# Adding attention masks on VectorE in the pass that takes the row minimum, and giving the compressed keys a matmul in common with the local branch

## The chip, the cores and the metric

The kernel runs on one core of one Trainium2 chip. The metric is device time in microseconds (us) from launch to end of one execution; the median of several runs is compared. Engines are named as the profile names them: PE is TensorE (PEld its weight loads), DVE is VectorE, ACT is ScalarE, POOL is GpSimd and SP the engine that issues most transfers.

## What is computed

The program is a two-layer decoder trunk over 1024 tokens of width 1024. Layer 0 is a convolution path with memory attention, and an MLP. Layer 1 has three-branch sparse attention (NSA) with memory attention, and an MLP. The change lies in the three branches of layer 1. For a block c of 128 queries, t the query's position:

```python
s = einsum('bqghd,bngd->bqghn', qb, k_cmp) * scale             # compressed keys: 63, in 64 columns
p_cmp = masked_softmax(s, cmp_end[None, :] <= t[:, None])
...
smask = (top_val > -inf)[..., None] & (pos <= t[...])          # selected blocks
p = masked_softmax(s_selected, smask)
...
wmask = (kp <= t) & (kp > t - WIN) & (kp >= 0)                 # sliding window of 512
p = masked_softmax(s_window, wmask)
o = o_cmp * gate[0] + o_slc * gate[1] + o_win * gate[2]
```

With 16 blocks of 64 keys and 16 selected, the selected branch holds every key up to the query, so it is plain causal attention here.

## The kernel before

Tokens are worked on in two halves of 512 (`hf` 0 and 1). After layer 0 has been done for half 0, the program calls `attend(0)`, then the output projection and MLP of layer 0 for half 1, then `attend(1)`, and after it the output projection and MLP of layer 1 for both halves. Each `attend` ends in `nsa`, the stage that the change touches.

A scheduler lays out each engine's order when the program is built: it takes the steps in program order with estimated durations and lets independent ones pass. So the matmuls of an MLP (`mlp`: L441 to L443 into `ps_i`, L81 to L83 into `ps_mo`) stand between those of `nsa` on PE. Each engine then executes its row of instructions in that order.

`nsa` walks 8 memory-attention units and then 24 units per half: 2 key groups g, 4 query blocks c in descending order, 3 head pairs j. A unit has two heads i. `scores` computes one unit: for each head it multiplies the query by the keys. Every query is split into a high and a low part that fill the 128 rows, so each stretch of keys takes two matmuls (x is 0 or 1) into one bank of `ps_s` (three banks). The pieces of a unit are S (selected keys, at most 512 columns a piece: S0, S1), W (window keys: W0, W1) and C (64 compressed keys).

Masks are added on PE. `nsa_masks` builds `far` (128 columns, the window's far edge) and `dcm` (for each c 128 columns of diagonal mask, then 64 of compressed mask). A piece with a mask gets one more matmul into the same bank, with the identity `ident_r` as weights and the mask as the moving operand. In the pieces `dC` one mask matmul of 192 columns covers the window's diagonal and the compressed keys at once.

Then, for each piece, DVE takes the negated row maximum out of PSUM (L983), ACT does the exponential with it as bias, and sums the row (L987). After that DVE works out scale factors in the tile `small` (L990 to L1000) and POOL multiplies the probabilities by them (L1002, L1006). `values` then transposes the probabilities on PE (L1020), ACT and DVE split them into high and low parts (L1024, L1028), and PE multiplies them by V (L1036, L1039). The values of one unit follow the scores of the next.

The MLP's weights are prepared in slices of 128x512: a DMA brings a slice, ACT writes its high part (L109) and POOL its low part (L110).

Of the kernel before, what the change touches and what calls it, by code (L numbers as in the profile page):

```python
# [8 lines left out]
F32 = mybir.dt.float32  # L9
F32R = mybir.dt.float32r  # L10
# [853 lines left out]

def nsa_masks(k, far, dcm):

    nc = k.nc
    with k.tc.tile_pool(name="mb", bufs=1, side="right") as mp:  # L870
        z = mp.tile([P, P], F32, name="z")
        f = mp.tile([P, 2, P], F32, name="f")
        d = mp.tile([P, 8, 64], F32, name="d")
        nc.gpsimd.memset(z, 0.0)
        nc.gpsimd.affine_select(f[:, 0], z, [[1, P]], compare_op=ALU.is_ge, fill=NEG, base=-1, channel_multiplier=-1)
        nc.gpsimd.tensor_copy(far, f[:, 0])
        nc.gpsimd.affine_select(f[:, 1], z, [[-1, P]], compare_op=ALU.is_ge, fill=NEG, base=0, channel_multiplier=1)
        nc.gpsimd.tensor_copy(dcm[:, :, 0:P], f[:, 1:2].to_broadcast([P, 8, P]))
        nc.gpsimd.memset(d, NEG)
        for c in range(8):  # L880
            if c < 4:
                nc.gpsimd.affine_select(d[:, c, 0:31], z[:, :31], [[-16, 31]], compare_op=ALU.is_ge, fill=NEG,
                                        base=128 * c - 31, channel_multiplier=1)
            else:
                nc.gpsimd.memset(d[:, c, 0:31], 0.0)
                nc.gpsimd.affine_select(d[:, c, 32:64], z[:, :32], [[-16, 32]], compare_op=ALU.is_ge, fill=NEG,
                                        base=128 * c - 527, channel_multiplier=1)
        nc.gpsimd.tensor_copy(dcm[:, :, P:], d)


def nsa(k, pool, psum, hf, q, mq, gate, KcS, Vc, masks, Kd, Vd, kvd, pslot, mem_dst, out):


    nc = k.nc
    far, dcm = masks
    n = 4 * hf + 4
    outv = out.rearrange("(a p) k t -> p a k t", a=2)
    ring = [0]
# [38 lines left out]
    def scores(Q, c, g, j, KS, V):  # L937


        nb = min(c, 4) + 1  # L940
        Ws, Ww = (c + 1) * P, nb * P
        ko = (c + 1 - nb) * P
        h0 = 6 * g + 2 * j
        nm, ls, r, mn, f = small()
        sm = pool.tile([P, 2, 256], F32, tag="sm", name="sm", bufs=3)
        dia, cm = dcm[:, c, 0:P], dcm[:, c, P:]


        C = (KcS[:, g], sm[:, :, 128:192], [(0, cm)], 0)
        dC = (KcS[:, g], sm[:, :, 128:192], [(-P, dcm[:, c])], 0)  # L950
        if hf == 0:
            Sp, Wp = p4(), p4()
            S = (KS[:, 0, 0:Ws], Sp, [(Ws - P, dia)], 1)
            W = (KS[:, 1, 0:Ww], Wp, [(Ww - P, dia)] if c == 3 else [], 3)
            chunks = [[S, W, dC]] if c == 0 else [[S], [W, dC]] if c < 3 else [[S], [W], [C]]
            parts = [(Sp[:, :, :Ws], 0, 0), (Wp[:, :, :Ww], 1, 0)]
            sel = [Sp[:, :, b * P:(b + 1) * P] for b in range(c + 1)]
            win = [Wp[:, :, b * P:(b + 1) * P] for b in range(nb)]
        else:
            Sa, Wp, Sb = p4(), p4(), p4()  # L960
            S0 = (KS[:, 0, 0:HF], Sa, [], 1)
            S1 = (KS[:, 0, HF:Ws], Sb, [(Ws - HF - P, dia)], 2)
            W0 = (KS[:, 1, ko:ko + HF], Wp, [(0, far)], 3)
            W1 = (KS[:, 1, c * P:c * P + P], sm, [], 4)
            chunks = [[S0], [W0], [S1, W1, dC]] if c < 6 else [[S0], [S1], [W0], [W1, dC]]
            parts = [(Sa, 0, 0), (Sb[:, :, :Ws - HF], 0, 1), (Wp, 1, 0), (sm[:, :, 0:P], 1, 1)]
            sel = [(Sa if b < 4 else Sb)[:, :, b % 4 * P:b % 4 * P + P] for b in range(c + 1)]
            win = [Wp[:, :, b * P:(b + 1) * P] for b in range(4)] + [sm[:, :, 0:P]]
        for i in range(2):
            for chunk in chunks:  # L970
                ps = bank()
                mms, at, where = [], 0, []
                for keys, _, ms, _ in chunk:
                    w = keys.shape[-1]
                    mms += [(at, w, Q[:, x, i * P:(i + 1) * P], keys) for x in range(2)]
                    mms += [(at + a, m.shape[-1], k.ident_r, m) for a, m in ms]
                    where.append((at, at + w))
                    at += w
                for n_, (a, w, lhs, rhs) in enumerate(mms):
                    nc.tensor.matmul(ps[:, a:a + w], lhsT=lhs, rhs=rhs, start=(n_ == 0), stop=(n_ == len(mms) - 1))  # L980
                for (a, b), (_, dst, _, ix) in zip(where, chunk):
                    m = nm[:, ix, i:i + 1]
                    nc.vector.tensor_reduce(m, ps[:, a:b], axis=AX.X, op=ALU.max, negate=True)  # L983
                    if c == 0 and ix == 0:
                        nc.vector.tensor_scalar(m, m, 1e29, None, op0=ALU.min)
                    l = ls[:, ix, i:i + 1] if hf == 1 and ix else r[:, (ix + 1) // 2, i:i + 1]
                    nc.scalar.activation(dst[:, i, 0:b - a], ps[:, a:b], AF.Exp, bias=m, accum_out=l)  # L987
        if hf == 1:
            nv, lv = (t[:, 1:5].rearrange("p (b x) i -> p b x i", b=2) for t in (nm, ls))
            nc.vector.tensor_tensor(mn, nv[:, :, 0], nv[:, :, 1], op=ALU.min)  # L990
            nc.vector.tensor_sub(f, mn[:, :, None, :].to_broadcast([P, 2, 2, 2]), nv)
            nc.scalar.activation(f, f, AF.Exp)
            nc.vector.tensor_mul(lv, lv, f)
            nc.vector.tensor_add(r[:, 1:3], lv[:, :, 0], lv[:, :, 1])
# [50 lines left out]
    def units():  # L1045
        KS = pool.tile([P, 4, 256], F32R, tag="KS", name="KSm", bufs=1)
        V = pool.tile([P, 2, 4, P], F32R, tag="V", name="Vm", bufs=1)
        nc.sync.dma_start(KS.bitcast(F32), kvd[:, 0:1024].rearrange("p (h t) -> p h t", h=4))
        nc.sync.dma_start(V.bitcast(F32), kvd[:, 1024:2048].rearrange("p (t h d) -> p t h d", t=2, h=4))
        for cp in range(2):  # L1050
            for h in range(4):
                yield mem_query, mem_scores, (cp, h, KS, V)
        for g in range(2):
            KS = pool.tile([P, 2, 1024], F32R, tag="KS", name="KS", bufs=1)
            V = pool.tile([P, 2, 8, P], F32R, tag="V", name="V", bufs=1)
            nc.sync.dma_start(KS[:, :, :n * P].bitcast(F32), Kd[:, g, :, :n * P])
# [57 lines left out]
def build(tc, ins, out):  # L1114
# [11 lines left out]
    with ExitStack() as es:  # L1126
# [4 lines left out]
        nc.sync.dma_start(k.cols, ins["cols"])  # L1131
        k.ident = cp.tile([P, P], F32, name="ident")
        make_identity(nc, k.ident)
        k.ident_r = cp.tile([P, P], F32R, name="ident_r")
        nc.gpsimd.tensor_copy(k.ident_r, k.ident)
        k.ones = cp.tile([P, P], F32, name="ones")
        nc.gpsimd.memset(k.ones, 1.0)
        halves = cp.tile([P, 24], F32, name="halves")
# [91 lines left out]

        ka = K()
        ka.nc, ka.tc, ka.i = nc, tc, ins
        ka.cols, ka.rows, ka.ident, ka.ident_r, ka.ones = k.cols, k.rows, k.ident, k.ident_r, k.ones
        ka.mqg, ka.kng = k.mqg, k.kng
        ka.lo_eng = nc.vector
        ka.nraw, ka.nhl, ka.tag, ka.nps, ka.nc_, ka.nt_ = NRAWA, NHLA, "a", 4, 3, 2
# [122 lines left out]
```

## Time and profile before

| what | value |
|---|---|
| median of 3 runs | 2488.69 us (2487.76 to 2490.86) |
| the profiled execution | 2490.74 us |
| its span, first to last instruction | 2488.9 us |
| mean granted PE clock | 0.987 of full speed |
| PE busy | 2410.1 us, 97% of the span, 12566 matmuls |
| DVE busy | 1667.7 us, 67%, 3270 instructions |
| ACT busy | 1294.0 us, 52% |
| POOL busy | 1223.6 us, 49% |

The profile's busy time is the union of an engine's records. A matmul's record is longer than the time by which it delays the next one, since matmuls overlap; what one costs is read from the chain of waits, which lists how much each piece moves the end. Line numbers are those of the kernel before unless said otherwise.

### The profile page before, as it was taken

To read this page: it belongs to the slowest core of one execution; us is meant where nothing else is said; L and a number is where in the kernel's file an instruction comes from. 1 tells how busy PE (TensorE), PEld (TensorE's weight loads), DVE (VectorE), ACT (ScalarE), POOL (GpSimd) and SP (SyncE) were. 2 spreads that over 40 slices of the span, in tenths; PEclk is the share of its full clock that TensorE was granted. 3 is DMA by queue.
4 is the path that set the end of the run, shared out by engine and by line. 5 is a ranking of instruction groups with operands and counts; after the bars stand their busy time and mean duration, and the time that the engine had idled before them with its cause. 6 is when DMAs were issued, how large, how long until landed. Compare 5 with 4: busy or idle time off the path is not lost.

```text
span 2488.9 us, 37416 instructions
## 1 busy us (share of the span) xinstructions
PE 2410.1 (97%) x12566; PEld 2043.2 (82%) x12566; DVE 1667.7 (67%) x3270; ACT 1294.0 (52%) x2938; POOL 1223.6 (49%) x1044
## 2 busy tenths in 40 slices
PE   7997999999998999999999999999999999999999
PEld 5886788888787888888787898888888887888887
DVE  7898587987778666766436866777777655433333
ACT  5565555333545466665334545666666644333332
POOL 3675743556632356464445325555555542444443
PEclk9998999999999999999999999999999999999999
DMA  6311433232444242322335434212222124332323
GB/s 212 100 50 53 140 104 104 93 101 92 140 140 130 89 117 69 89 70 84 109 102 164 145 112 125 82 57 59 71 80 60 56 82 147 119 97 93 98 94 102
DMA packets 157791, 250.91 MB, mean 101 GB/s; under 512 B 17696, under 2 KB 49056, under 8 KB 157088
## 3 DMA queue, kind: packets, MB, share of 16 engines
q1 hardware_dynamic: 157600, 248.52, 32.2%
q8 instruction: 100, 1.64, 0.3%
q14 instruction: 91, 0.75, 0.1%
HBM read 217.52 MB, written 20.45 MB: 96 GB/s over the span
## 4 chain that ended last, share of the span: by engine, by line
PE 64%; DVE 4%; DMA 2%; issue 1%; ACT 1%; POOL 1%; SPq 0%; ACTq 0%; DVEq 0%; POOLq 0%
PE ps_mo L81 7%; PE ps_i L441 7%; PE ps_i L443 7%; PE ps_i L442 7%; PE ps_mo L83 7%; PE ps_mo L82 7%; PE ps_s L980 6%; PE ps_t L1020 4%; PE ps_o L1036 2%; PE ps_o L1039 2%; PE ps_tok L666 1%; PE ps_tok L668 1%; PE ps_tok L667 1%; PE ps_wo L400 1%; PE ps_wo L402 1%
## 5 line engine op out<-in xcount | busy, mean ns | idle before, releaser
L110 POOL TENSOR_TENSOR hl<-raw,hl 128x512 fp32r<-128x512 f32 x592 | 771.4, 1313 | 938.3 <-ACT hl L109 901.5
L109 ACT ACTIVATE hl<-raw 128x512 fp32r<-128x512 f32 x656 | 409.8, 630 | 647.5 <-PE ps_mo L83 248.3
L463 DVE TENSOR_TENSOR x<-x,ps_mo 128x512 f32<-128x512 f32 x512 | 348.5, 683 | 157.0 <-PE ps_mo L83 154.2
L81 PE MATMUL ps_mo<-hid,hl 128*128 128x512 f32 x1024 | 410.9, 402 | 9.2 <-DVE a L449 5.6
L441 PE MATMUL ps_i<-act,hl 128*128 128x512 f32 x1024 | 406.3, 397 | 8.5 <-DVE x L404 6.9
L442 PE MATMUL ps_i<-act,hl 128*128 128x512 f32 x1024 | 404.5, 395 | 1.2 <-DVE act L410 1.2
L443 PE MATMUL ps_i<-act,hl 128*128 128x512 f32 x1024 | 404.8, 396 | 0.0
L83 PE MATMUL ps_mo<-hid,hl 128*128 128x512 f32 x1024 | 402.8, 393 | 0.0
L82 PE MATMUL ps_mo<-hid,hl 128*128 128x512 f32 x1024 | 402.2, 393 | 0.0
L81 PEld LDWEIGHTS ps_mo<-hid,hl 128*128 128x128 f32 x1024 | 193.0, 189 | 51.9 <-DVE x L463 7.8
L441 PEld LDWEIGHTS ps_i<-act,hl 128*128 128x128 f32 x1024 | 193.3, 189 | 48.4 <-DVE x L404 7.3
L442 PEld LDWEIGHTS ps_i<-act,hl 128*128 128x128 f32 x1024 | 193.1, 189 | 42.5 <-DVE act L410 2.2
L83 PEld LDWEIGHTS ps_mo<-hid,hl 128*128 128x128 f32 x1024 | 192.9, 188 | 41.0
L443 PEld LDWEIGHTS ps_i<-act,hl 128*128 128x128 f32 x1024 | 193.1, 189 | 40.6 <-issue 0.2
L82 PEld LDWEIGHTS ps_mo<-hid,hl 128*128 128x128 f32 x1024 | 193.2, 189 | 37.0 <-issue 0.7
L449 DVE SCALAR_TENSOR_TENSOR a<-ps_i,r 128x512 f32<-128x512 f32 x128 | 87.9, 688 | 196.4 <-PE ps_i L443 192.0
L983 DVE TENSOR_REDUCE small<-ps_s 128x1 f32<-128x512 f32 (+4 forms) x384 | 164.0, 442 | 51.8 <-PE ps_s L980 35.9
L987 ACT ACTIVATE prob<-ps_s,small 128x512 f32<-128x512 f32 (+3 forms) x240 | 141.1, 589 | 98.8 <-DVE small L983 96.6
L1028 DVE TENSOR_TENSOR PT<-ps_t,PT 128x512 fp32r<-128x512 f32 (+1 forms) x220 | 146.8, 671 | 65.9 <-ACT PT L1024 64.6
L1006 POOL TENSOR_TENSOR prob<-prob,small 128x1024 f32<-128x1024 f32 (+3 forms) x120 | 180.9, 1532 | 1.1 <-DVE small L1000 0.7
L1024 ACT ACTIVATE PT<-ps_t 128x512 fp32r<-128x512 f32 (+1 forms) x256 | 140.8, 566 | 69.9 <-PE ps_t L1020 65.7
L980 PE MATMUL ps_s<-KS,Q 128*128 128x512 f32 (+3 forms) x576 | 148.3, 349 | 0.0
(299 smaller groups left out, 4781.9 us busy)
## 6 DMA issues: line engine op xcount, KB each, us to landing
raw<-in_w_mlp_in_dram SPq DMA_DIRECT2D x256, 256.0 KB, 2.7
raw<-in_w_mlp_out_dram SPq DMA_DIRECT2D x256, 256.0 KB, 2.8
raw<-in_w_out_dram SPq DMA_DIRECT2D x64, 256.0 KB, 3.0
Q<-Q SPq DMA_DIRECT2D x160, 64.0 KB, 2.0
raw<-in_cmp_w_dram SPq DMA_DIRECT2D x32, 256.0 KB, 2.7
raw<-in_a_w_dram SPq DMA_DIRECT2D x24, 256.0 KB, 2.8
raw<-in_b_wq_dram SPq DMA_DIRECT2D x24, 256.0 KB, 2.7
mixd<-ev SPq DMA_DIRECT2D x80, 64.0 KB, 2.1
```

The lines of the kernel that those rows point to most:

```text
L81: nc.tensor.matmul(ps, lhsT=lh, rhs=rh, start=(i == 0), stop=False)
L82: nc.tensor.matmul(ps, lhsT=lh, rhs=rl, start=False, stop=False)
L83: nc.tensor.matmul(ps, lhsT=ll, rhs=rh, start=False, stop=(i == n - 1))
L109: nc.scalar.activation(hl[:, 0, :n], raw[:, :n], AF.Copy)
L110: k.last_lo = k.lo_eng.tensor_tensor(hl[:, 1, :n], raw[:, :n], hl[:, 0, :n].bitcast(F32), op=ALU.subtract)
L441: nc.tensor.matmul(p_, lhsT=wh, rhs=h[kt][:, 0], start=kt == 0, stop=False)
L442: nc.tensor.matmul(p_, lhsT=wh, rhs=h[kt][:, 1], start=False, stop=False)
L443: nc.tensor.matmul(p_, lhsT=wl, rhs=h[kt][:, 0], start=False, stop=kt == KT - 1)
L463: nc.vector.tensor_add(x[o], x[o], ps)
L980: nc.tensor.matmul(ps[:, a:a + w], lhsT=lhs, rhs=rhs, start=(n_ == 0), stop=(n_ == len(mms) - 1))
L983: nc.vector.tensor_reduce(m, ps[:, a:b], axis=AX.X, op=ALU.max, negate=True)
L1006: nc.gpsimd.tensor_tensor(t, t, sc[:, :, None].to_broadcast([P, 2, t.shape[-1]]), op=ALU.mult)
```

## The change

Masks go to DVE. A masked piece is now handled by one operation, `tensor_tensor_reduce`: it reads scores from PSUM and a mask from SBUF, writes minus their sum back to the same place of PSUM, and takes the minimum of the row (starting from 1e29) into `small`. The exponential then reads the negated scores with scale -1. In the instruction stream the operation is two instructions: the pass itself (`ISA ps_s,small<-ps_s,...`) and a second one that writes the row's result (`ISA small 128x1`). Pieces without a mask keep the plain reduction.

`edge` holds both 128-column masks in one f32 tile of 640 columns: far, then 384 columns of zeros, then the diagonal, so a slice of it gives a mask as wide as the piece. `cm` holds the compressed masks. `ident_r`, and the casts of masks for PE, are gone.

The window's keys in `KS` are followed by 64 compressed keys, which POOL copies there at the first head pair of each (g, c) (16 copies); c descends, so the block that they overwrite is no longer needed. W and C are then one moving operand. For c of 0 and 4 a strided operand also takes the diagonal block of the selected keys, with 64 columns between them that are computed and not read.

```diff
-        dia, cm = dcm[:, c, 0:P], dcm[:, c, P:]
-        C = (KcS[:, g], sm[:, :, 128:192], [(0, cm)], 0)
-        dC = (KcS[:, g], sm[:, :, 128:192], [(-P, dcm[:, c])], 0)
+        win0 = 1024
+        last = KS[:, win0 + c * P:win0 + c * P + P + 64]
+        if j == 0:
+            nc.gpsimd.tensor_copy(last[:, P:], KcS[:, g])
+        C = (64, sm[:, :, 128:192], cm[:, c], 0)
         if hf == 0:
...
-            chunks = [[S, W, dC]] if c == 0 else [[S], [W, dC]] if c < 3 else [[S], [W], [C]]
+            chunks = [[(KS[:, 0:Ws], [S])]]
+            chunks += [[(KS[:, win0:win0 + Ww + 64], [W, C])]] if c < 3 else [
+                [(KS[:, win0:win0 + Ww], [W])], [(last[:, P:], [C])]]
         else:
...
-            chunks = [[S0], [W0], [S1, W1, dC]] if c < 6 else [[S0], [S1], [W0], [W1, dC]]
+            chunks = [[(KS[:, 0:HF], [(HF, Sa, None, 1)])], [(KS[:, win0 + ko:win0 + ko + HF], [W0])]]
+            end = [(KS[:, HF:Ws], [S1]), (last, [W, C])]
+            chunks += [end] if c == 5 else [end[:1], end[1:]]
...
+        if c % 4 == 0:
+            both = KS[:, 0:2 * win0].rearrange("p (a t) -> p a t", a=2)[:, :, c * P:c * P + P + 64]
+            chunks[0 if hf == 0 else 2:] = [[(both, [tri, (64, None, None, None), W, C])]]
...
-                    mms += [(at + a, m.shape[-1], k.ident_r, m) for a, m in ms]
...
-                    nc.vector.tensor_reduce(m, ps[:, a:b], axis=AX.X, op=ALU.max, negate=True)
-                    if c == 0 and ix == 0:
-                        nc.vector.tensor_scalar(m, m, 1e29, None, op0=ALU.min)
+                    if mask is None:
+                        nc.vector.tensor_reduce(m, s, axis=AX.X, op=ALU.max, negate=True)
+                    else:
+                        nc.vector.tensor_tensor_reduce(s, s, mask, -1.0, 1e29, ALU.add, ALU.min, m)
                     l = ls[:, ix, i:i + 1] if hf == 1 and ix else r[:, (ix + 1) // 2, i:i + 1]
-                    nc.scalar.activation(dst[:, i, 0:b - a], ps[:, a:b], AF.Exp, bias=m, accum_out=l)
+                    nc.scalar.activation(dst[:, i, 0:w], s, AF.Exp, bias=m, scale=1.0 if mask is None else -1.0, accum_out=l)
```

Counted over the instruction streams, the score matmuls go from 1020 to 552. Of 576 on keys, 192 on compressed keys and 252 on masks there remain 264 of 512 columns (unchanged), 24 of 448, 96 of 384, 24 of 320, 48 of 256, 72 of 192 and 24 of 64. On DVE 336 of the 384 reductions become pairs (144 in half 0, 192 in half 1), and 12 small `tensor_scalar` go.

Three places show how the order moves. The first is PE in half 1, a unit of c = 6, one head: its S1 (384 columns), W0, W1 and C. Before:

```order
L980 MATMUL ps_s<-KS,Q 128x384 x2
L980 MATMUL ps_s<-dcm,ident_r 128x128
L980 MATMUL ps_s<-KS,Q 128x512 x2
L980 MATMUL ps_s<-far,ident_r 128x128
L980 MATMUL ps_s<-KS,Q 128x128 x2
L980 MATMUL ps_s<-KcS_2539,Q 128x64 x2
L980 MATMUL ps_s<-dcm,ident_r 128x192
```

The same pieces of such a unit after the change (`ps_o` and `ps_t` belong to the unit before it):

```order
L989 MATMUL ps_s<-KS,Q 128x512 x2
L1052 MATMUL ps_o<-PT,V 128x256
L1049 MATMUL ps_o<-PT,V 128x256
L1052 MATMUL ps_o<-PT,V 128x256
L1033 MATMUL ps_t<-ident,prob 128x128 x4
L989 MATMUL ps_s<-KS,Q 128x384 x2
L989 MATMUL ps_s<-KS,Q 128x192 x2
```

Eleven matmuls have become six. Between the first and the last score matmul of half 0 the order now has 615 MLP matmuls of 512 columns where it had 534, and in half 1 it has 1091 where it had 961; after the last one 2023 PE rows remain, before 2156.

The second place is DVE in half 1, at a unit of c = 4. Before, with the split of transposed probabilities (L1028) between the reductions:

```order
L1028 TENSOR_TENSOR PT<-ps_t,PT 128x512
L983 TENSOR_REDUCE small<-ps_s 128x1
L1028 TENSOR_TENSOR PT<-ps_t,PT 128x512
L983 TENSOR_REDUCE small<-ps_s 128x1 x2
L1028 TENSOR_TENSOR PT<-ps_t,PT 128x512
L983 TENSOR_REDUCE small<-ps_s 128x1
```

After (S0 has no mask, W0 has the far mask, S1 the diagonal):

```order
L1041 TENSOR_TENSOR PT<-ps_t,PT 128x512
L995 TENSOR_REDUCE small<-ps_s 128x1
L449 SCALAR_TENSOR_TENSOR a<-ps_i,r 128x512
L998 ISA ps_s,small<-ps_s,edge 128x512
L998 ISA small 128x1
L998 ISA ps_s,small<-ps_s,edge 128x128
L998 ISA small 128x1
```

Each masked piece takes two places in the queue where it took one.

The third place is POOL in half 1, where a new query block begins. Such a copy had no counterpart before:

```order
L1019 TENSOR_TENSOR prob<-prob,small 128x1024
L1019 TENSOR_TENSOR sm<-sm,small 128x2x128
L110 TENSOR_TENSOR hl<-raw,hl 128x512 x2
L945 COPY KS<-KcS_2537 128x64
L1015 TENSOR_TENSOR sm<-sm,small 128x2x64
```

The copy waits for PE (the last window matmul of the block before) and stands behind two preparations of weights; the first window matmul of the new block waits for it.

## Rows read from the trace of the kernel before

**Rows 1.** The page: busy us of the engines, and PE in 40 slices.

```profile
PE 2410.1 (97%) x12566; PEld 2043.2 (82%) x12566; DVE 1667.7 (67%) x3270; ACT 1294.0 (52%) x2938; POOL 1223.6 (49%) x1044
...
PE   7997999999998999999999999999999999999999
```

**Rows 2.** Windows, the two attention stages: us, then busy us of PE, PEld, DVE, ACT, POOL.

```profile
911.00:1136.00 225.00, 225.00 (x1383) 200.19 (x1382) 163.39 (x383) 155.99 (x456) 125.24 (x126) 1.00 0.27 77
1556.00:1998.00 442.00, 442.00 (x2669) 390.50 (x2667) 328.95 (x734) 293.17 (x818) 251.32 (x219) 1.00 0.22 66
```

**Rows 3.** Chain of waits: its shares by line, then pieces: start, us, what.

```profile
by line: PE ps_mo L81 6.8%; PE ps_i L441 6.7%; PE ps_i L443 6.7%; PE ps_i L442 6.6%; PE ps_mo L83 6.6%; PE ps_mo L82 6.6%; PE ps_s L980 5.7%; PE ps_t L1020 4.2%; PE ps_o L1036 2.3%; PE ps_o L1039 2.1%; PE ps_tok L666 1.4%; PE ps_tok L668 1.
...
1133.04 1.54 PE ps_s L980 x14
...
1566.68 1.10 PE ps_s L980 x8
...
1699.52 0.46 PE ps_s L980 x2
1699.98 0.23 PE ps_mo L81
1700.21 0.53 PE ps_s L980 x3
1700.74 0.28 PE ps_mo L82
...
1701.48 0.88 PE ps_s L980 x8
```

**Rows 4.** Groups by form, DVE from 1560 to 2000 us: count, busy us, mean ns.

```profile
L1028 DVE TENSOR_TENSOR PT<-ps_t,PT 128x512 fp32r<-128x512 f32 x119 | 81.3, 685 | 38.1 <-ACT PT L1024 37.3
L983 DVE TENSOR_REDUCE small<-ps_s 128x1 f32<-128x512 f32 x105 | 71.6, 683 | 17.9 <-PE ps_s L980 17.3
L463 DVE TENSOR_TENSOR x<-x,ps_mo 128x512 f32<-128x512 f32 x80 | 54.3, 680 | 8.4 <-PE ps_mo L83 7.5
L89 DVE TENSOR_TENSOR hid<-a,hid 128x512 fp32r<-128x512 f32 x20 | 17.4, 872 | 9.2 <-ACT hid L88 8.8
L983 DVE TENSOR_REDUCE small<-ps_s 128x1 f32<-128x128 f32 x59 | 16.4, 283 | 8.1 <-PE ps_s L980 6.5 <-ACT prob L987 1.4
L449 DVE SCALAR_TENSOR_TENSOR a<-ps_i,r 128x512 f32<-128x512 f32 x20 | 13.7, 683 | 3.8 <-PE ps_i L443 3.7
...
L983 DVE TENSOR_REDUCE small<-ps_s 128x1 f32<-128x64 f32 x46 | 9.9, 216 | 4.4 <-ACT sm L987 4.2
```

**Rows 5.** Timeline of DVE, then of ACT, from 1700 us: start, us, engine, line.

```profile
1700.94 0.69 DVE L1028 TENSOR_TENSOR PT<-ps_t,PT 128x512 fp32r<-128x512 f32 x1
1701.54 0.68 DVE L983 TENSOR_REDUCE small<-ps_s 128x1 f32<-128x512 f32 x1
1702.14 0.68 DVE L1028 TENSOR_TENSOR PT<-ps_t,PT 128x512 fp32r<-128x512 f32 x1
...
1703.45 0.69 ACT L987 ACTIVATE prob<-ps_s,small 128x512 f32<-128x512 f32 x1 [3.20 <-DVE small L983]
1704.04 0.19 ACT L987 ACTIVATION_READ_ACCUMULATOR prob<-ps_s,small 128x1 f32 x1
1704.16 0.69 ACT L987 ACTIVATE prob<-ps_s,small 128x512 f32<-128x512 f32 x1
```

**Rows 6.** Waits from 1560 to 2000 us: total us, times, longest us.

```profile
POOL hl L110 <- ACT hl L109: 144.0, 37, 8.9
ACT prob L987 <- DVE small L983: 65.7, 56, 4.3
```

**Rows 7.** Groups by form: preparation of a weight slice, and a small POOL pass.

```profile
L110 POOL TENSOR_TENSOR hl<-raw,hl 128x512 fp32r<-128x512 f32 x592 | 771.4, 1313 | 938.3 <-ACT hl L109 901.5 <-issue 33.0 <-DVE nt L97 1.8
...
L109 ACT ACTIVATE hl<-raw 128x512 fp32r<-128x512 f32 x656 | 409.8, 630 | 647.5 <-PE ps_mo L83 248.3 <-PE ps_i L443 244.3 <-PE ps_wo L402 26.9
...
L1002 POOL TENSOR_TENSOR sm<-sm,small 128x128 f32<-128x128 f32 x96 | 41.0, 428 | 93.2 <-DVE small L998 73.8 <-PE ps_s L226 5.7 <-ACT PT L1024 5.3
```

More of the change, by code (lines that the diff above doesn't have):

```diff
@@ L862, in kv_tok, with nsa_masks @@
     k.pe(850)
-def nsa_masks(k, far, dcm):
+def nsa_masks(k, edge, cm):
     nc = k.nc
[L870 to L888, printed above, removed]
+    z = edge[:, P:2 * P]
+    nc.gpsimd.memset(edge[:, P:4 * P], 0.0)
+    nc.gpsimd.affine_select(edge[:, 0:P], z, [[1, P]], compare_op=ALU.is_ge, fill=NEG, base=-1, channel_multiplier=-1)
+    nc.gpsimd.affine_select(edge[:, 4 * P:], z, [[-1, P]], compare_op=ALU.is_ge, fill=NEG, base=0, channel_multiplier=1)
+    nc.gpsimd.memset(cm, NEG)
+    for c in range(8):
+        if c < 4:
+            nc.gpsimd.affine_select(cm[:, c, 0:31], z[:, :31], [[-16, 31]], compare_op=ALU.is_ge, fill=NEG,
+                                    base=128 * c - 31, channel_multiplier=1)
+        else:
+            nc.gpsimd.memset(cm[:, c, 0:31], 0.0)
+            nc.gpsimd.affine_select(cm[:, c, 32:64], z[:, :32], [[-16, 32]], compare_op=ALU.is_ge, fill=NEG,
+                                    base=128 * c - 527, channel_multiplier=1)
 def nsa(k, pool, psum, hf, q, mq, gate, KcS, Vc, masks, Kd, Vd, kvd, pslot, mem_dst, out):
     nc = k.nc
-    far, dcm = masks
+    edge, cm = masks
     n = 4 * hf + 4
@@ L945, in scores @@
         sm = pool.tile([P, 2, 256], F32, tag="sm", name="sm", bufs=3)
-        dia, cm = dcm[:, c, 0:P], dcm[:, c, P:]
-        C = (KcS[:, g], sm[:, :, 128:192], [(0, cm)], 0)
-        dC = (KcS[:, g], sm[:, :, 128:192], [(-P, dcm[:, c])], 0)
+        win0 = 1024
[3 more added lines that the diff above has]
+        C = (64, sm[:, :, 128:192], cm[:, c], 0)
         if hf == 0:
             Sp, Wp = p4(), p4()
-            S = (KS[:, 0, 0:Ws], Sp, [(Ws - P, dia)], 1)
-            W = (KS[:, 1, 0:Ww], Wp, [(Ww - P, dia)] if c == 3 else [], 3)
-            chunks = [[S, W, dC]] if c == 0 else [[S], [W, dC]] if c < 3 else [[S], [W], [C]]
+            S = (Ws, Sp, edge[:, 5 * P - Ws:], 1)
+            W = (Ww, Wp, edge[:, 5 * P - Ww:], 3)
             parts = [(Sp[:, :, :Ws], 0, 0), (Wp[:, :, :Ww], 1, 0)]
@@ L958, in scores @@
             win = [Wp[:, :, b * P:(b + 1) * P] for b in range(nb)]
+            chunks = [[(KS[:, 0:Ws], [S])]]
+            chunks += [[(KS[:, win0:win0 + Ww + 64], [W, C])]] if c < 3 else [
+                [(KS[:, win0:win0 + Ww], [W])], [(last[:, P:], [C])]]
+            tri = S
         else:
             Sa, Wp, Sb = p4(), p4(), p4()
[L961 to L964, printed above, removed]
-            chunks = [[S0], [W0], [S1, W1, dC]] if c < 6 else [[S0], [S1], [W0], [W1, dC]]
+            S1 = (Ws - HF, Sb, edge[:, 5 * P - Ws + HF:], 2)
+            W0 = (HF, Wp, edge[:, 0:HF], 3)
+            W = (P, sm, edge[:, 4 * P:], 4)
+            chunks = [[(KS[:, 0:HF], [(HF, Sa, None, 1)])], [(KS[:, win0 + ko:win0 + ko + HF], [W0])]]
+            end = [(KS[:, HF:Ws], [S1]), (last, [W, C])]
+            chunks += [end] if c == 5 else [end[:1], end[1:]]
             parts = [(Sa, 0, 0), (Sb[:, :, :Ws - HF], 0, 1), (Wp, 1, 0), (sm[:, :, 0:P], 1, 1)]
@@ L968, in scores @@
             win = [Wp[:, :, b * P:(b + 1) * P] for b in range(4)] + [sm[:, :, 0:P]]
+            tri = S1
+        if c % 4 == 0:
+            both = KS[:, 0:2 * win0].rearrange("p (a t) -> p a t", a=2)[:, :, c * P:c * P + P + 64]
+            chunks[0 if hf == 0 else 2:] = [[(both, [tri, (64, None, None, None), W, C])]]
         for i in range(2):
@@ L971, in scores @@
                 ps = bank()
[L972 to L975, printed above, removed]
-                    mms += [(at + a, m.shape[-1], k.ident_r, m) for a, m in ms]
[L977 to L982, printed above, removed]
-                    nc.vector.tensor_reduce(m, ps[:, a:b], axis=AX.X, op=ALU.max, negate=True)
-                    if c == 0 and ix == 0:
-                        nc.vector.tensor_scalar(m, m, 1e29, None, op0=ALU.min)
+                at, mms, where = 0, [], []
+                for keys, pieces in chunk:
+                    b = at
+                    for piece in pieces:
+                        where.append((b, piece))
+                        b += piece[0]
+                    out_ = ps[:, at:b]
+                    if len(keys.shape) == 3:
+                        out_ = out_.rearrange("p (a t) -> p a t", a=2)
+                    mms += [(out_, Q[:, x, i * P:(i + 1) * P], keys) for x in range(2)]
+                    at = b
+                for n_, (o_, lhs, rhs) in enumerate(mms):
+                    nc.tensor.matmul(o_, lhsT=lhs, rhs=rhs, start=(n_ == 0), stop=(n_ == len(mms) - 1))
+                for a, (w, dst, mask, ix) in where:
+                    if dst is None:
+                        continue
+                    m, s = nm[:, ix, i:i + 1], ps[:, a:a + w]
+                    if mask is None:
+                        nc.vector.tensor_reduce(m, s, axis=AX.X, op=ALU.max, negate=True)
+                    else:
+                        nc.vector.tensor_tensor_reduce(s, s, mask, -1.0, 1e29, ALU.add, ALU.min, m)
                     l = ls[:, ix, i:i + 1] if hf == 1 and ix else r[:, (ix + 1) // 2, i:i + 1]
-                    nc.scalar.activation(dst[:, i, 0:b - a], ps[:, a:b], AF.Exp, bias=m, accum_out=l)
+                    nc.scalar.activation(dst[:, i, 0:w], s, AF.Exp, bias=m, scale=1.0 if mask is None else -1.0, accum_out=l)
         if hf == 1:
@@ L1053, in units @@
         for g in range(2):
-            KS = pool.tile([P, 2, 1024], F32R, tag="KS", name="KS", bufs=1)
+            KS = pool.tile([P, 2 * 1024 + 64], F32R, tag="KS", name="KS", bufs=1)
+            kv2 = KS[:, 0:2048].rearrange("p (b t) -> p b t", b=2)
             V = pool.tile([P, 2, 8, P], F32R, tag="V", name="V", bufs=1)
-            nc.sync.dma_start(KS[:, :, :n * P].bitcast(F32), Kd[:, g, :, :n * P])
+            nc.sync.dma_start(kv2[:, :, :n * P].bitcast(F32), Kd[:, g, :, :n * P])
             nc.sync.dma_start(V[:, :, :n].bitcast(F32), Vd[:, g, :, :n])
@@ L1133, in build @@
         make_identity(nc, k.ident)
-        k.ident_r = cp.tile([P, P], F32R, name="ident_r")
-        nc.gpsimd.tensor_copy(k.ident_r, k.ident)
         k.ones = cp.tile([P, P], F32, name="ones")
@@ L1199, in build @@
         tail = late.tile([P, 4, 8], F32, name="tail")
-        masks = (late.tile([P, P], F32R, name="far"), late.tile([P, 8, 192], F32R, name="dcm"))
+        masks = (late.tile([P, 5 * P], F32, name="edge"), late.tile([P, 8, 64], F32, name="cm"))
         xp = pool(es, "x")
@@ L1232, in build @@
         ka.nc, ka.tc, ka.i = nc, tc, ins
-        ka.cols, ka.rows, ka.ident, ka.ident_r, ka.ones = k.cols, k.rows, k.ident, k.ident_r, k.ones
+        ka.cols, ka.rows, ka.ident, ka.ones = k.cols, k.rows, k.ident, k.ones
         ka.mqg, ka.kng = k.mqg, k.kng
```

## The prediction

> **What bounds the kernel now.** I read the page first, then the windows of the two stages that the change touches, then the chain of waits there. The page shows PE busy for 97% of the span and in nearly every slice [rows 1]. The windows say more: from the first score matmul to the last, 225 us in half 0 and 442 us in half 1, PE has no idle time at all, while DVE is busy for 163.4 and 329.0 us of them [rows 2]. The reader is to see that what keeps PE occupied there is not only attention: the order puts MLP matmuls between the pieces, so PE always has something to do. The chain of waits runs along PE through both stages, and 5.7% of it, some 142 us, is the line of the score matmuls [rows 3]. So work taken off PE there comes off the end, as long as the other engines still feed it. That is the whole argument, and DVE is the engine to watch, since it gets the work.
>
> **What PE loses.** The chain gives the price of a matmul as the time by which it moves the next. A 512-column one costs 0.23 us, two 0.46 [rows 3], which is 0.45 ns per column. A narrow one costs far more than its columns: fourteen of 64 to 192 columns in a row take 1.54 us, 0.11 each; two of 512 and six narrow ones take 1.10, again 0.11 for a narrow one; two of 256 and six narrow ones take 0.88. A single mask matmul behind two wide ones shows as 0.07 (0.53 less 0.46), but the wide matmul behind it then costs 0.28, so 0.12 in all [rows 3]. I price all widths up to 192 at 0.11 and the others by columns: 0.115 for 256, 0.144 for 320, 0.173 for 384, 0.202 for 448.
>
> Before, besides the 264 of 512 columns that stay: 612 narrow ones, 67.3 us; 72 of 256, 8.3; 72 of 384, 12.4; together 88.0 us. After: 24 of 448, 4.8; 96 of 384, 16.6; 24 of 320, 3.5; 48 of 256, 5.5; 96 narrow, 10.6; together 41.0 us. PE loses 47 us, about 19 in half 0 and 28 in half 1. As a check, the prices give 264 x 0.23 + 88.0 = 149 us for the line before, where the chain has 142. If all the difference lies in the narrow ones they cost 0.10 and the gain is 41 us. I keep 47 and hold 41 as its near end. The order agrees with a full PE: the scheduler fills the freed room with 81 and 130 more MLP matmuls, and those are missing later. Some 300 MLP matmuls of half 0 are still left behind the last unit, so the stage that follows keeps its cover.
>
> [...] The rows have a narrow matmul at 0.11 us [rows 3]. [...]
>
> **What DVE gains.** 336 reductions become a pass with two inputs and a readout. The pass: for 512 columns the reduction takes 683 ns and the nearest operation with one input in PSUM and one in SBUF takes 685 [rows 4], and in the timeline both follow each other at 0.60 us [rows 5]. So I take the pass at the reduction's price. The readout has no row on DVE. On ACT the same thing, an accumulator read behind the exponential, is a record of 0.19 us that delays the next instruction by 0.12 [rows 5]. I call the extra price per masked piece d and take d = 0.12. Its low end is 0: both forms read the same columns, and nothing suggests that the new one could be cheaper. Its high end is a sum and a reduction done one after the other. A reduction delays the next by its record less 0.08 (0.60 of 0.683 [rows 4, 5]), so 0.60, 0.20 and 0.14 us for 512, 128 and 64 columns; over the mix of half 1 the second pass is 0.33 on average, and with 0.15 for a readout as an operation of its own d = 0.48.
>
> [...]
>
> Room on DVE: the MLP's own DVE work comes to 54.3 + 17.4 + 13.7 us [rows 4] for 961 matmuls, 0.089 each, so the extra MLP matmuls add 7.2 us in half 0 and 11.6 in half 1. Free are then 225 - 163.4 - 7.2 = 54 us for 144 pieces, d = 0.38, and 442 - 329.0 - 11.6 = 101 us for 192, d = 0.53 [rows 2]. At d = 0.12 DVE gets 17 and 23 us, and is 83% busy. So it is hidden behind PE. But PE takes its row in a fixed order: a late maximum delays the exponential, and ACT already waits for DVE there 56 times, 4.3 us at the longest [rows 6]. If a bank of scores or a transposed block is late, PE stands. I charge 4 us for such stands; nothing in the trace prices them, and PE has none now.
>
> **The other edits.** ACT's count is unchanged. Sixteen copies on POOL cost at most 0.43 us each by a pass twice as wide [rows 7], and POOL is idle for 100 us in half 0 and 191 in half 1 [rows 2]. The transfers are the same. The copy adds a wait: the first window matmul of a block waits for POOL, and the copy stands behind weight preparations, which themselves wait for ACT, 8.9 us at the longest [rows 6]. About fifty PE rows lie between the matmul that frees the columns and the one that needs them, 8 us or so at 0.16 us each (442 us for 2669 [rows 2]), so I take it as hidden.
>
> **The sum.** 2490.7 - 47 + 4 = 2448 us for the profiled execution. The median of the runs is 2 us below that execution, so **2446 us** is the forecast, 1.7% faster. Each rival below is on the median's scale too.
>
> **Rivals.**
> - **DVE fills up in half 0.** With d = 0.48 half 0 has 144 x 0.48 = 69 us to place in 54, so 15 us come back, and half 1 is nearly full, with some 2 us of stands more: about 2463. For: DVE is the busiest of the three feeding engines, and nothing bounds a pass that writes PSUM and reads it. Against: the two-input row costs what the reduction costs.
> - **DVE becomes the bound and it is slower.** Per 0.1 of d over both limits 33.6 us come back. The gain of 47 is gone at 336 d - 155 = 47, d = 0.60. At d = 0.75, which is the second pass, the readout and 0.27 us more per pair, 49 us are lost: about 2538. For: the instruction is of a kind that the trace does not have, and most masked pieces are small, so a fixed cost per instruction would weigh twice. Against: a reduction of 64 columns takes 0.216 us in all [rows 4], so the fixed part of a DVE pass is small here.
> - **The copy is late.** If each of the sixteen holds PE for one weight preparation and itself, 0.63 + 1.31 + 0.43 = 2.4 us [rows 7], 38 us come back; half of them, 19, is more likely as the order has room: about 2465.
> - **Narrow matmuls are cheaper than they look, and the change does not take off what it should.** If a narrow one costs only the 0.07 us that the single mask matmul shows by itself [rows 3], the 516 fewer save 0.04 us less each, 21 us, and the gain is 26: about 2465 with no stands more. By columns alone, 33,800 fewer at 0.45 ns, it would be 15 us: about 2475. The rows of 1.54 and 1.10 us speak against both. [...]
>
> **Chances.** Forecast 0.70; DVE full in half 0 0.12; late copy 0.05; narrow matmuls cheaper 0.06; slower 0.07, of which 0.02 fall near d = 0.60 and count as no change. A measurement of this kernel tells about 0.2%, 5 us, from no change. So faster 0.93, same 0.02, slower 0.05. The range goes from 2436 (the 47 with no stands and 6 us to spare for idle stretches that change elsewhere) to 2474, which takes in the first and third rival and the nearer case of the fourth.
>
> **What would show it.** In the profile after: PE still without idle time in both attention stages; the score line's share of the chain near 100 us in place of 142; the pass for 512 columns near 690 ns and its readout under 0.2 us; DVE busy below 90% of the stages. Wrong would be waits of PE for DVE or ACT inside the stages, for POOL at a new block, or a pass above 1 us.

## The result, and the profile after

| what | before | after |
|---|---|---|
| median of the runs | 2488.78 us (4 runs) | 2461.36 us (2460.16 to 2463.82, 4 runs) |
| ratio, 95% interval | | 0.989 [0.9873, 0.9907] |
| span of the profiled execution | 2488.9 us | 2458.4 us |
| mean granted PE clock | 0.987 | 0.984 |

The kernel is 27.4 us faster, 1.1%. The forecast was 2446 us, so 15 us of the 43 that it promised are missing. One execution of experiment 4 below ran at a granted clock of 0.60 and took 3647.7 us; it is left out of that experiment's time. Line numbers in the views of a run are those of that run's kernel. The page after:

```profile
PE 2366.0 (96%) x12098; PEld 1995.2 (81%) x12098; DVE 1674.5 (68%) x3594; ACT 1293.9 (53%) x2938; POOL 1227.3 (50%) x1056
...
PE   7997999999988999999999999999999998899999
```

PE is busy 44.1 us less than before, but the span is only 30.5 us shorter [rows 1]: PE now idles 92.4 us where it idled 78.8. The two 8s near the end of its row (slices 34 and 35, some 2030 to 2150 us) were 9s.

**Inside the two stages the signs of the forecast came true.** Windows of the stages, columns as in [rows 2]:

```profile
911.00:1128.00 217.00, 217.00 (x1240) 189.58 (x1239) 166.43 (x500) 157.14 (x454) 130.80 (x135) 1.00 0.30 85
1544.00:1982.00 438.00, 438.00 (x2510) 381.81 (x2510) 346.26 (x938) 298.95 (x833) 265.25 (x235) 1.00 0.24 71
```

PE has no idle time in either; DVE is busy for 77 and 79% of them. In the chain of waits the score line fell from 5.7% of the span to 4.1%, from 142 to 101 us, and two 384-column matmuls show 0.35 us (the forecast had 0.173 each):

```profile
by line: PE ps_i L441 7.0%; PE ps_i L443 6.9%; PE ps_i L442 6.9%; PE ps_mo L81 6.3%; PE ps_mo L83 6.3%; PE ps_mo L82 6.3%; PE ps_t L1033 4.2%; PE ps_s L989 4.1%; PE ps_o L1049 2.3%; PE ps_o L1052 2.1%; issue 1.9%; PE ps_tok L666 1.5%; PE ps
...
1711.45 0.35 PE ps_s L989 x2
```

The new passes on DVE (`CUSTOM_DVE_ANT_0`) and their readouts, groups by form from 1540 to 1990 us, which answer to [rows 4]:

```profile
L1041 DVE TENSOR_TENSOR PT<-ps_t,PT 128x512 fp32r<-128x512 f32 x122 | 83.3, 685 | 22.1 <-ACT PT L1037 21.0
...
L998 DVE CUSTOM_DVE_ANT_0 ps_s<-ps_s,edge 128x512 f32<-128x512 f32 x58 | 40.0, 695 | 8.2 <-PE ps_s L989 7.6 <-PE ps_t L1033 0.3
L995 DVE TENSOR_REDUCE small<-ps_s 128x1 f32<-128x512 f32 x47 | 32.1, 683 | 8.4 <-PE ps_s L989 8.0
L998 DVE DVE_READ_ACCUMULATOR2_ANT small<- 128x1 f32 x190 | 25.9, 136 | 0.2
...
L998 DVE CUSTOM_DVE_ANT_0 ps_s<-ps_s,edge 128x128 f32<-128x128 f32 x60 | 18.0, 301 | 5.6 <-PE ps_s L989 4.8 <-ACT hid L88 0.5 <-ACT prob L1000 0.2
...
L998 DVE CUSTOM_DVE_ANT_0 ps_s<-ps_s,cm 128x64 f32<-128x64 f32 x48 | 10.8, 227 | 4.3 <-ACT sm L1000 3.9
```

A pass of 512 columns takes 695 ns beside 683 for the reduction, one of 128 columns 301 beside 283, one of 64 columns 227 beside 216. The readout has a record of 136 ns. The timeline of DVE, which answers to [rows 5], shows where this record stands:

```profile
1703.99 0.68 DVE L463 TENSOR_TENSOR x<-x,ps_mo 128x512 f32<-128x512 f32 x1
1704.59 0.69 DVE L998 CUSTOM_DVE_ANT_0 ps_s<-ps_s,edge 128x512 f32<-128x512 f32 x1
1705.20 0.14 DVE L998 DVE_READ_ACCUMULATOR2_ANT small<- 128x1 f32 x1
1705.20 0.33 DVE L998 CUSTOM_DVE_ANT_0 ps_s<-ps_s,edge 128x128 f32<-128x128 f32 x1
```

The next pass starts together with the readout, 0.61 us behind the start of the pass before, where two other operations are 0.60 apart. Its own record is 0.33 us, and 0.29 where a 128-column pass starts without a readout; splits of 512 columns (L1041) are 0.60 from start to start with a readout beside them or without. So d, the extra price per masked piece, is about 0.02 us, not 0.12.

**The time was lost behind the second stage.** PE in 10-us windows after the change, columns as in [rows 2] but PE alone, then its clock, DMA share and GB/s:

```profile
2020.00:2030.00 10.00, 8.18 (x35) 1.00 0.63 193
2030.00:2040.00 10.00, 4.36 (x18) 0.89 1.04 387
2040.00:2050.00 10.00, 7.26 (x21) 0.59 0.73 237
...
2090.00:2100.00 10.00, 4.17 (x11) 0.62 0.00 0
2100.00:2110.00 10.00, 9.32 (x29) 0.69 0.00 0
```

Before, the same part of the program (some 25 us later) has two shallow dips, and the list of waits below shows that in both PE waits with a matmul of the MLP, not with one of the projection or the norm:

```profile
2060.00:2070.00 10.00, 6.88 (x19) 0.66 0.76 230
...
2120.00:2130.00 10.00, 9.27 (x39) 1.00 0.43 142
```

What PE waits for, from 1980 to 2140 us (total us, times, longest). Before:

```profile
PE ps_mo L81 <- DVE a L449: 3.1, 1, 3.1
PE ps_mo L81 <- DVE x L463: 0.7, 1, 0.7
```

After:

```profile
PE ps_wo L400 <- ACT hl L109: 7.6, 1, 7.6
PE ps_n L164 <- DVE diag L156: 3.0, 1, 3.0
PE ps_n L150 <- DVE acc L140: 2.9, 1, 2.9
PE ps_mo L81 <- DVE x L463: 2.6, 2, 1.3
PE ps_i L441 <- ACT r L420: 0.7, 1, 0.7
```

The chain of waits after the change, at the first hole:

```profile
2020.17 0.43 DVE ev L1055
2020.61 2.07 DMA mixd<-ev
...
2023.61 5.15 DMA mix<-mixd
...
2031.80 5.43 DMA out_dram<-x
2037.29 4.74 DMA raw<-in_w_out_dram
2042.05 0.64 ACT hl L109
2042.74 0.79 PE ps_wo L400
2043.53 0.43 PE ps_wo L401
...
2048.22 0.24 PE ps_wo L400
```

Both kernels have this sequence: the last attention result goes out to memory (`mixd`) and comes back, behind that SP issues the load of the output projection's first weight slice, ACT prepares it, and then PE can start the projection. From the last store to the issue of that load it takes 16.7 us after the change and 16.2 before. What differs is what PE has to do meanwhile, its cover: MLP matmuls that need none of this. The order of PE behind the last value matmul, in numbers of matmuls (each of the norm's leaves two records in the trace):

```
before: MLP 84, projection 14, MLP 5, projection 2, MLP 1, projection 176, MLP 18, norm 4, MLP 30, norm 1, MLP 12, then half 1
after:  MLP 54, projection 192, norm 4, norm 1, then half 1
```

Before, 150 MLP matmuls of half 0 stand there, 60 of them around the norm (12 more stand a little later, among the first of half 1's MLP); now 54, and none around the norm. The missing ones were drawn forward into half 1's attention, where the removed matmuls made room.

And the hole costs more than its idle time: the eleven matmuls behind the first take 0.43 us each, not 0.24, in a stretch whose granted clock is 0.59 of full speed. PE had stood for 7.6 us just before. The same happens once more behind the norm (waits of 2.9, 3.0 and 0.7 us, then a matmul of the MLP and eleven more at 0.43 us each), at granted clocks of 0.62 and 0.69. Before, there is one such stretch, behind the wait of 3.1 us (twelve at 0.43 us, clock 0.66), so one of the two is new.

### The profile page after: what moved, and what is told of

Same layout as the page of the kernel before. It is cut to its first block, busy times and chain, and to the rows that moved or that the text cites. A ratio compares the mean times of both kernels' runs of the same rounds, so it can differ in the third digit from the quotient of the medians.

```text
span 2458.4 us, 36789 instructions
## 1 busy us (share of the span) xinstructions
PE 2366.0 (96%) x12098; PEld 1995.2 (81%) x12098; DVE 1674.5 (68%) x3594; ACT 1293.9 (53%) x2938; POOL 1227.3 (50%) x1056
## 4 chain that ended last, share of the span: by engine, by line
PE 63%; DVE 4%; DMA 2%; issue 2%; POOL 1%; ACT 1%; SPq 0%; ACTq 0%; POOLq 0%; DVEq 0%
PE ps_i L441 7%; PE ps_i L443 7%; PE ps_i L442 7%; PE ps_mo L81 6%; PE ps_mo L83 6%; PE ps_mo L82 6%; PE ps_t L1033 4%; PE ps_s L989 4%; PE ps_o L1049 2%; PE ps_o L1052 2%; PE ps_tok L666 1%; PE ps_tok L667 1%; PE ps_tok L668 1%; PE ps_wo L400 1%; PE ps_wo L402 1%
## 5 line engine op out<-in xcount | busy, mean ns | idle before, releaser
L1041 DVE TENSOR_TENSOR PT<-ps_t,PT 128x512 fp32r<-128x512 f32 (+1 forms) x220 | 147.0, 671 | 48.2 <-ACT PT L1037 46.6
L989 PE MATMUL ps_s<-KS,Q 128*128 128x512 f32 (+5 forms) x552 | 143.0, 358 | 0.0
L89 DVE TENSOR_TENSOR hid<-a,hid 128x512 fp32r<-128x512 f32 x128 | 100.7, 788 | 58.8 <-ACT hid L88 58.2
```

The costliest lines, as they stand in the source:

```text
L989: nc.tensor.matmul(o_, lhsT=lhs, rhs=rhs, start=(n_ == 0), stop=(n_ == len(mms) - 1))
L1041: nc.vector.tensor_sub(PT[:, 1, :m], Tv[:, :m], PT[:, 0, :m].bitcast(F32))
```

## Experiments

Each run's "before" is the kernel before on the same chip, 2488.65 us for the first four, 2490.18 for the next four and 2489.27 for the last four, 9 runs each. The change itself was not measured again in these sets: where a run is compared with it, or with a run of another set, the gains against "before" are compared, each good to some 3 or 4 us either way. My theory after the result: PE's relief is as forecast, but half 1's attention swallows the cover of the stage behind it. The rivals: narrow matmuls are worth less than 0.11 us, or the new DVE passes cost something that the windows hide.

**1. The change in half 0 alone** (`yield query, scores if hf in (0,) else scores_old`, with the masks of either kind for its half).

> The change in half 0 only; half 1 keeps the masks and compressed keys of the kernel before. Theory (PE sheds its matmuls at 0.11 us each in both stages; the shortfall lies behind half 1's attention, where the MLP matmuls that covered the wait for the output projection have been used up): half 0's 19 us arrive whole, the stretch behind half 1's attention stays as in the kernel before; 2488.8 - 19 = about 2470 us, PE idle behind the last attention matmul some 9 us as before. Rival A (narrow matmuls are cheaper than 0.11 us, so the whole gain is smaller everywhere): 19 x 27/47 = 11 us, about 2478. Rival B (the new DVE operation holds the stage up): gain clearly under 19 us, with idle PE inside half 0's attention stage.

2471.43 us, ratio 0.9929 [0.9916, 0.9943]: 17.2 us faster, for 19 forecast. PE's order behind the second stage is the one of before, and so are its waits there (3.2 and 0.7 us in all).

**2. The change in half 1 alone.**

> The change in half 1 only; half 0 keeps the kernel before. Theory: of half 1's 28 us some 16 to 20 are lost behind the attention, so 8 to 12 us remain: about 2477 to 2481 us, with some 14 us more of idle PE between the last attention matmul and the MLP of half 1 than before, and TensorE's granted clock lower there. Rival A (cheaper narrow matmuls): 28 x 27/47 = 16 us, about 2473. Rival B (DVE holds the stage up): idle PE inside half 1's attention stage.

2480.91 us, ratio 0.9964 [0.9951, 0.9976]: 7.7 us faster, for 28 forecast. 54 MLP matmuls are left, as in the whole change, and PE's waits there are the same:

```profile
PE ps_wo L400 <- ACT hl L109: 7.7, 1, 7.7
PE ps_mo L81 <- DVE x L463: 3.0, 2, 1.7
PE ps_n L164 <- DVE diag L156: 3.0, 1, 3.0
PE ps_n L150 <- DVE acc L140: 2.9, 1, 2.9
...
```

So the loss belongs to half 1. Half 0's gain arrives whole: the first score matmul of half 1 starts 18.2 us earlier in run 1 than before (1495.7 for 1513.9). That this is so because more MLP follows half 0 fits the order, but no run tests it.

**3. The change, with 144 MLP matmuls held back.** From step 14 of half 0's MLP on, every PE instruction is placed behind the last value matmul of half 1. That is about the cover of before (144 for 150):

```diff
+    with ExitStack() as held:
         for c in range(NC):
+            if c == at:
+                held.enter_context(k.tc.issue_after(hold.ins))
             nxt = proj_in(c + 1) if c + 1 < NC else None
```

> The change, and besides 144 MLP matmuls of half 0 (the last output slice but one, the last input and output slices) are queued on PE behind the last attention matmul of half 1. Theory, in its strong form (the scheduler fills freed PE time greedily, and the attention of half 1 needs no more than PE's own time): the stretch behind the attention is covered again, about 2445 to 2450 us. Weak form (half 1's attention has a length of its own, set by the other engines' steps, that PE's lighter load does not shorten): the 90 matmuls taken out of the stage leave about as much idle PE inside it as they save behind it, 2455 to 2465 us. Rivals A and B (loss elsewhere): no change against the changed kernel, 2461 us, and no less idle PE behind the attention.

**2446.64 us**, ratio 0.9829 [0.9816, 0.9843]: 42.0 us faster than before; the median is 14.7 us below that of the change. The matmuls are the same, only their order differs. The row from 1980 to 2140 us, of the change and then of this kernel:

```profile
1980.00:2140.00 160.00, 143.30 (x647) 116.31 (x646) 72.21 (x129) 60.84 (x110) 48.98 (x39) 0.93 0.35 111
```

```profile
1980.00:2140.00 160.00, 153.91 (x716) 126.06 (x714) 80.47 (x141) 67.54 (x123) 55.71 (x43) 0.99 0.38 120
```

The idle time falls by 10.6 us (16.7 to 6.1), and PE's busy time on the page by 4.8 (2366.0 to 2361.2) with the same matmuls, while the granted clock of the row rises from 0.93 to 0.99. Together that is 15.4 us, beside 13.3 between the two profiled spans (2458.4 and 2445.1) and 14.7 between the medians, so the account holds to some 2 us.

**4. The change without any mask** (`mask = None`: plain reductions, and the output is attention without masks).

> The change without any attention mask: the shared matmuls stay, and every piece has the plain reduction, so DVE has neither the new pass nor its readout. It leaves the masks out of the computation. Theory (the new pass costs DVE next to nothing that counts): same time as the changed kernel within 4 us, 2457 to 2465, and the same idle PE behind the attention. Rival B (DVE's new pass costs what is missing): about 2445, 15 us or more faster than the changed kernel. Rival A: no change either.

2466.2 us (three executions), ratio 0.9905 [0.989, 0.992], not faster than the change and 1 us above the range expected. The 336 passes and readouts cost nothing on the path that this run can tell. The hole is there as well, and with 42 MLP matmuls left PE waits longer in it for the projection (10.3 us for 7.6), which could hide a gain of some 3 us; experiment 8 takes that away.

**5. Only the masks on DVE, and 144 held.** The compressed keys keep matmuls of their own:

```diff
-            end = [(KS[:, HF:Ws], [S1]), (last, [W, C])]
+            m2, m3, m4 = (KS[:, HF:Ws], [S1]), (KS[:, win0 + c * P:win0 + c * P + P], [W]), (KcS[:, g], [C])
```

> Half of the change, with the 144 held matmuls: masks are added on VectorE, but the compressed keys keep matmuls of their own (no copy behind the window's keys, no shared operand). 252 mask matmuls go, 192 of 64 columns stay. If a narrow matmul costs 0.11 us, 27.7 us come off: 2461 us, and PE stays full in both stages. If it costs the 0.07 us that a single one shows, 17.6 us come off: 2471. If the pass and its readout on VectorE cost anything that counts, this kernel shows it in full and lands above 2471 with idle time of PE inside the stages.

2466.77 us, ratio 0.9904 [0.9891, 0.9918]: 23.4 us for 252 matmuls, 0.093 each (0.081 to 0.108 by the interval). That lies between the two prices. The trace of before agrees: from 1514 to 1980 us a narrow matmul on keys or masks starts 0.10 us ahead of the next one on average, but 0.06 with the 128 columns of `far` and 0.17 with the 192 of `dcm`, so one price for all widths was a simplification. PE has no idle time from 1535 to 1980 us.

**6. Only the sharing of keys, and 144 held.** Masks stay matmuls:

```diff
+                        if mask is not None:
+                            mms.append((ps[:, a + mask[0]:a + mask[0] + mask[1].shape[-1]], k.ident_r, mask[1]))
```

> The other half of the change, with the 144 held matmuls: W and C share a matmul and a strided operand takes the diagonal block with them, but masks are added by 252 matmuls on PE as before, and VectorE has plain reductions. 216 matmuls fewer than before. By 0.11 us for a narrow one and columns for the wider ones the change's 47 us less 27.7 are left: 2469 us. If narrow ones cost 0.07, 26 less 17.6 are left: 2480. If the two halves are additive, their gains together make the 42 us of the run with the whole change and the held matmuls.

2474.25 us, ratio 0.9936 [0.9924, 0.9949]: 15.9 us, between the two times expected. At the 0.093 of run 5 for a narrow matmul, 264 fewer save 24.6 and the wider ones take 9.7 back (30.4 for 20.7), 14.9 in all. The halves make 39.3 together, beside 42.0 for the whole; with intervals of some 3 us either way on each they are additive as far as can be told.

**7. 240 held instead of 144.**

> The change with 240 instead of 144 MLP matmuls of half 0 held behind the last attention matmul. If what the hole behind the attention costs is all given back by 144, more cover changes nothing: 2444 to 2448 us. If the few us of idle time that are left there (some 7 us between 1980 and 2080 us) are still for want of cover, 2440 to 2444. If the 72 matmuls fewer inside half 1's attention leave PE without work there, idle time appears inside that stage and it is slower: 2450 to 2460.

2452.62 us, ratio 0.985 [0.9837, 0.9864], 4 to 7 us worse than 144 (37.6 us faster than before; runs 3 and 10 have 42.0 and 44.1). The third case: the stage has no work to give away. From 1535 to 1980 us PE now idles:

```profile
1535.00:1980.00 445.00, 441.70 (x2547) 384.03 (x2545) 352.81 (x962) 306.28 (x852) 265.51 (x238) 1.00 0.24 72
```

and what it waits for from 1900 us on is attention's own pipeline:

```profile
PE ps_t L1036 <- DVE PT L1044: 2.6, 3, 0.9
PE ps_mo L81 <- DVE a L449: 2.4, 1, 2.4
PE ps_o L1055 <- DVE PT L1044: 1.4, 4, 0.7
```

**8. No masks, and 144 held.**

> The change with the 144 held matmuls and no masks at all: every piece has the plain reduction, so the 336 two-input passes and readouts are gone, and what is computed is attention without masks. PE's matmuls are the same. If the passes on VectorE are hidden, it is as fast as with them: 2445 to 2449 us. If each of them costs the path anything (0.01 us for 336 is 3.4 us; my forecast charged 4 us), it is faster by that: 2442 or less.

2449.39 us, ratio 0.9836 [0.9823, 0.985], beside 0.9829 with masks: the same. With the hole covered too, the passes on DVE cost nothing that can be told.

**9. The stores of half 0's result on ACT's queue,** without held matmuls. In the changed kernel they stand on SP ahead of the first load for the output projection:

```diff
-            mlp(k, 1, x[hf], act[hf], rs[hf], lambda o: nc.sync.dma_start(out[hf, :, o], x[hf][o]))
+            mlp(k, 1, x[hf], act[hf], rs[hf], lambda o: (nc.sync if hf else nc.scalar).dma_start(out[hf, :, o], x[hf][o]))
```

> The change as it is, without held matmuls; only the eight stores of half 0's result (L1301) go to ACT's queue instead of SP's. In the changed kernel they stand on SP ahead of the first load of the output projection's weights, and each waits for the last MLP matmuls of half 0. If PE's longest wait in the hole (8.4 us for the first prepared weight slice of the output projection) comes from that, the load is issued earlier and 5 to 8 us come back: 2453 to 2456 us. If the slots of raw weights, or the attention result's way out and back, hold it, nothing changes: 2459 to 2463.

2465.0 us, ratio 0.9902 [0.9888, 0.9915], no gain (2 us above the range expected for that case). The chain above names a store just ahead of the load, but the load is no earlier without it:

```profile
2025.07 0.59 SPq L1056 DMA_DIRECT2D mixd<-ev  x1
2027.21 1.28 SPq L380 DMA_DIRECT2D mix<-mixd  x3
...
2043.76 13.72 SPq L106 DMA_DIRECT2D raw<-in_w_out_dram  x8
```

18.7 us from the last attention store to the load, where the change has 16.7. So the stores are not the cause, and this reading of the chain falls. Whether the buffers for raw slices or the way of the attention result out and back sets those 17 us was not tried further.

**10. The same, with 144 held.**

> The same move of the eight stores, with the 144 held matmuls. If the held matmuls already cover the wait for the output projection, the move changes nothing: 2445 to 2448 us. If the idle time that is left there (some 5 us) is the stores' doing, 2442 or less.

2445.2 us, ratio 0.9827 [0.9814, 0.984]: as without the move. But for the eight stores it is also a second measurement of 3, on another set of runs: 44.1 us faster than before.

**11. 96 held** (the hold starts one input slice later).

> The change with 96 held matmuls (output slices of the last two steps of half 0's MLP). 42 more than the changed kernel leaves by itself, 9.7 us of PE's work at 0.23 each, placed ahead of and inside the output projection; the norm behind it still has only 12 to cover it. If the hole is a want of cover and nothing else, about 9 us of the 15 come back: 2451 to 2454 us, and the norm's waits stay. If any cover at all is enough to keep the clock and the queue going, it is as fast as with 144: 2447.

2454.53 us, ratio 0.9865 [0.9851, 0.988]: 7 us better than the change, 7 to 9 worse than 144, about what a mere want of cover would give (9 us were expected). The wait for the projection is gone, the norm's is not:

```profile
PE ps_n L164 <- DVE diag L156: 4.3, 1, 4.3
PE ps_mo L81 <- DVE x L463: 2.9, 3, 1.4
...
PE ps_wo L400 <- ACT hl L109: 0.5, 1, 0.5
```

**12. 192 held.**

> The change with 192 held matmuls; 24 fewer inside half 1's attention than the order there would take. With 144 no idle time showed in that stage, with 240 (72 fewer inside) 5 us did. If the best lies where cover behind and work inside are both enough, this is at the flat bottom: 2445 to 2449 us. If the stage has no matmul to spare, a third of the 6 us by which 240 is slower is lost: 2448 to 2450.

2450.81 us, ratio 0.9846 [0.9833, 0.986], 4 to 6 us worse than 144, the second case or a little more. PE is thin already at the end of the stage:

```profile
1970.00:1980.00 10.00, 8.32 (x49) 1.00 0.15 53
1980.00:1990.00 10.00, 8.65 (x64) 1.00 0.07 13
1990.00:2000.00 10.00, 8.32 (x60) 1.00 0.04 8
```

With 144 held PE is busy for 10.00, 10.00 and 7.78 us of the same three windows, so it too runs thin there, but later. The difference also shows within the profiles: from the first score matmul of half 1 (memory units included) to the end, runs 7 and 12 take 953.9 us each, runs 3 and 10 949.9 and 949.8.

So over matmuls of half 0 held behind the stage the gain against before reads: 54 (the change) 27.4 us, 96: 34.7, 144: 42.0 and 44.1, 192: 38.5, 240: 37.6. The best of these, 144, beats the kernel before and the change.

## Why the prediction was right, and where it was wrong

Range and sign held, but a third of the gain was missing, and that the range held is in part luck: it reaches to 2474 us for three rivals, and none of them is what happened. The measured 2461 lies within 4 us of all three (2463 to 2465), and the windows and runs 3, 5 and 8 rule their causes out. The fourth rival's times were added up from the profiled execution; on the median's scale they are 2463 and 2474 in place of 2465 and 2475. By the prediction's own steps:

- **PE is full in both stages, so work taken off it comes off the end:** right inside the stages, where PE idles neither before nor after. It is shown by experiments 1, 3, 5 and 6, all of which take matmuls away and gain by it.
- **A narrow matmul costs 0.11 us, 47 us in all; 0.10 and 41 us as the near end:** right in kind, and in size the near end. The chain's share fell by 41 us; under cover 42.0 and 44.1 us came off, with some 2 us more idle time behind the stage than before (6.1 for 3.85 us). Masks alone gave 0.093 each, 0.081 to 0.108 by the interval; the 42.0 us under cover are 39 to 46 by theirs.
- **d = 0.12 us, DVE busy by 83%:** wrong in size, on the harmless side. The pass costs 11 to 18 ns more than the reduction at 512, 128 and 64 columns, and its readout of 136 ns overlaps the next operation, so d is about 0.02 and DVE stays below 80%. The rivals in which DVE fills up or becomes the bound fall; runs 4 and 8 show that without the passes nothing is gained.
- **4 us of stands for late maxima:** wrong, on the harmless side; PE has none in the stages.
- **Copies hidden on POOL:** right. POOL waits for PE there (`POOL KS L945 <- PE ps_s L989`, 12.2 us over the span), PE never for POOL in the stages, where it has no idle time.
- **"Some 300 MLP matmuls of half 0 are still left behind the last unit, so the stage that follows keeps its cover":** this is the step that failed. Counted behind the last score matmul, 298 is the number in the order before. The sentence before it said that 130 more go into the stage; 298 less 130 is 168, and 114 of these stand among the values of the last units. What covers the way out of the attention and the norm is 54, where it was 150. I took a count from before the move and used it after. The price of that is 14.7 us, measured by putting the cover back (run 3). In half 1 alone 20 us less than forecast arrived (run 2); some 3 of them are the price of a narrow matmul (28 x 42/47 is 25).

So with the forecast's PE gain at 42 rather than 47, no stands in place of 4, and 15 us for the lost cover, the sum is 27, which is what was measured. That is bookkeeping and no test, since 42 and 15 both come from run 3; runs 1 and 2, which do not, make 17.2 + 7.7 = 24.9 us. None of the rivals described this: each put the loss inside the stages or into the price of a matmul. The signs named in advance looked only there too: no idle PE, the score line at 101 us, the pass at 695 ns, DVE below 80% all came true while 15 us were lost elsewhere.

The scheduler is not at fault in a simple way. It let the MLP fill the freed room early, which is right as long as something else is left for later. Runs 3, 7, 11 and 12 show a best point between: too few behind the stage and PE stands at the projection and the norm, too many and it stands at the end of attention.

## What to carry to other kernels

Where a scheduler keeps an engine busy with filler, as here with MLP matmuls, work that is removed is replaced by filler from later, and the gain shows only where that filler runs out. So count, in the order after the change, what is left at the next places where the engine must wait (a round trip through memory, a norm), and reserve filler for them; how much is a number to try, since a stage that gives too much away stands itself. A gap can also cost more than its length: behind the 7.6 us here eleven matmuls ran at 0.43 us in place of 0.24.

## What was not expected of the hardware

The readout of a row result on DVE (136 ns on average) starts together with the next operation where one is ready, 0.61 us behind the start of a 512-column pass, for 0.60 without one, and a 128-column pass that starts beside it takes 0.33 us in place of 0.29, while the accumulator read on ACT that I had taken as its model delays the next by 0.12 us [rows 5]. And a two-input pass that reads 512 columns of PSUM, adds a mask from SBUF, writes them back and reduces them takes 695 ns, 12 more than the reduction that only reads.
